# Context's activations and retention's normalised tokens at byte 192 of a 256-byte line

## The chip, the cores and the metric

One core of a Trainium2 chip runs the whole program. The metric is the device time of one execution in microseconds (us); the time before is the median of three runs. The profile is of one further execution of the same program.

## What is computed

Two layers of a diffusion backbone over 512 latent tokens with 256 context tokens, width 1024, all in float32. Layer 0 is windowed attention, layer 1 a bidirectional retention; behind each mixer stands a SwiGLU feed-forward of inner width 2816. Context runs through layer 0 and its feed-forward, and in layer 1 only feeds retention's keys and values.

```python
def swiglu(h, w_in, w_out):
    gate, up = jnp.split(h @ w_in, 2, axis=-1)
    return (jax.nn.silu(gate) * up) @ w_out

...
x = x + mx[5] * swiglu(modulate(rms_norm(x, norm2_g[i]), mx[3], mx[4]), ffn_w_in[i], ffn_w_out[i])
if need_ctx_out:
    y_ctx = y_ctx + mc[2] * out_c
    y_ctx = y_ctx + mc[5] * swiglu(modulate(rms_norm(y_ctx, norm2_g[i]), mc[3], mc[4]),
                                   ffn_w_in[i], ffn_w_out[i])
...
q_x, k_x, v_x, g_x = jnp.split(h_x @ w_qkvg, [qk, 2 * qk, 2 * qk + RET_VWIDTH], axis=-1)
k_c, v_c = jnp.split(h_c @ w_qkvg[:, qk:2 * qk + RET_VWIDTH], [qk], axis=-1)
```

## The kernel before

Every dense product is made from three matmuls (`mm3`, L144): each float32 operand is split into a rounded high part and the remainder, and TensorE adds high x high, low x high and high x low. Numbers on both sides are of the type float32r. So 128 x 128 weights are loaded into the array (an LDWEIGHTS, "PEld" in the profile) for each matmul, and a stream of 128, 256, 384 or 512 columns passes through. Splitting costs a cast on ScalarE and a subtraction on VectorE.

**The first feed-forward** (L970 to L1316). Its 22 inner tiles of 128 features go through in groups of 2, 4, 4, 4, 4, 4. The 768 tokens (512 latent, then 256 context, `WIDE`) are computed in two halves of 384 (`THIRDS`). From the third tile on `seven` (L1129) makes gate and up projection with seven products of 384 columns (L994) on sums of tokens and weights instead of eight. `finish_half` (L1079) multiplies gate and up, writes the rounded half into an `act` tile (ScalarE, L1082) and the remainder behind it (VectorE, L1083). An `act` tile has 2 x 768 columns: high parts of latent and context, then low parts of latent and context. Context's high part stands at column 512 and its low part at column 1280, which are both multiples of 256 bytes.

`output` (L1214) applies the output weights of a finished group while the next group is being made: for each of eight output tiles first the latent tokens (512 columns into the bank pair `pj`, 3 matmuls a tile of the group), then the context tokens (256 columns into `Z`); `out_products` (L1206) takes the high and low parts by the offset `WIDE`. `last_output` (L1227) does the last group in three passes of 256 columns: first latent half, context, second latent half, with the squares for the next norm on ScalarE and, for context, their sums on GpSimd (L211).

**Retention** (L1324 on). Latent tokens are normalised and split into `h_first` and `h_rest` (tiles `aq`, L1334 and L1335) and their sums into `h_sum` (tiles `sA`, L1332); context into tiles `hc` (`context_norm`, L1400, by `norm_mod`, L246). For each of four heads `product_q` (L1408, its matmul L1415) makes queries and keys: the tokens are streamed, 256 columns at a time, over loaded weights. `product_v` (L1419, its matmul L1428) makes values and gates: the tokens are the loaded operand, 128 columns at a time, and 512 columns of weights are streamed. In a head the order on TensorE is: products of `aq` and `hc` by key weights (96 matmuls of L1415), of `sA` (96), of `aq` (24), then the value and gate products of L1428 with `aq`, `hc` and `sA`, in between the scores.

**Where a tile stands.** A pool hands out a partition's bytes in the order of first use. `off_grid(pool, 48)` (L226) takes 48 columns of float32, 192 bytes, so that the tiles after it start 192 bytes past a multiple of 256; `off_grid(pool, 16)` brings it back to the grid with 64 bytes more. Before the change this is done for attention's context tokens (L447), for `h_sum` (L1331) and for the second feed-forward's tokens `hx` (L1783), but not for the first feed-forward's `act`, nor for retention's `aq` and `hc`; these start at byte 0.

Each engine works through its own queue in order. `after(a, b)` (L91) places `a` behind `b` on an engine without a semaphore; `rounded[0]` (L1161) keeps the rounding of a tile's second half behind the next tile's first copy.

Of the kernel before, what the change touches and what calls it, by code (L numbers as in the profile page):

```python
# [9 lines left out]
F32R = mybir.dt.float32r  # L10
# [6 lines left out]
KT = D // P  # L17
SX = 512
SC = 256
# [30 lines left out]
def dit_kernel(ctx, tc, xT, cT, crow, small, consts, masks, tabs0, tabs1, jtab, adaQ, adaN, adaT, wst, out):  # L50
    nc = tc.nc
    mult, add, sub = ALU.mult, ALU.add, ALU.subtract
# [9 lines left out]
    def T(pool, cols, tag, bufs, dt=F32):  # L62
        return pool.tile([P, cols], dt, tag=tag, bufs=bufs, name=tag)

    def pj(n=512):
# [11 lines left out]
    acol = {(l, s, w): cp.tile([P, 8], F32, name=f"acol{l}{s}{w}")  # L77
            for l, s, w in ((0, 0, 0), (0, 1, 0), (0, 0, 1), (0, 1, 1), (1, 0, 0), (1, 1, 0), (1, 0, 1))}
# [12 lines left out]
    def after(ins, others):  # L91
        for o in others:
            tc.add_manual_dep(ins.ins, o.ins.name, order, reason="table set turn")
# [50 lines left out]
    def mm3(o, w, x, first, last, behind=()):  # L144

        whi, wlo = w
        xhi, xlo = x
        after(nc.tensor.matmul(o, whi, xhi, start=first, stop=False), behind)  # L148
        nc.tensor.matmul(o, wlo, xhi, start=False, stop=False)  # L149
        return nc.tensor.matmul(o, whi, xlo, start=False, stop=last)  # L150
# [70 lines left out]
    hpool = [None]  # L221
# [4 lines left out]
    def off_grid(pool, cols):  # L226

        nc.gpsimd.memset(T(pool, cols, "off%d" % cols, 1), 0.0)

    def h_tiles(s):  # L230
        hi = t_h(s)
        if s == 0:
            return hi, t_h(s)
        return hi[:, 0:SC], hi[:, SC:2 * SC]

    def modulate(l, s, which, k, res, h, c=slice(None), t=None, behind=()):
        y = ssq[s][:, c]
        if t is None:
            t = t_hn(y.shape[1])
        after(nc.vector.scalar_tensor_tensor(t, res[k][:, c], acol[l, s, which][:, k:k + 1], y, mult, mult), behind)  # L240
        hi, lo = h[0][:, c], h[1][:, c]
        b = mods[l, s][:, 3 * which, k:k + 1]
        nc.scalar.activation(hi, t, AF.Identity, bias=b)
        return nc.vector.scalar_tensor_tensor(lo, t, b, hi, add, sub)

    def norm_mod(l, s, which, res):  # L246
        h = []
        for k in range(KT):
            h.append(h_tiles(s))
            last = modulate(l, s, which, k, res, h[k])  # L250
        return h, last

    def gated_add(s, l, part, d, o, res):
        return nc.vector.scalar_tensor_tensor(res[d], o, mods[l, s][:, part, d:d + 1], res[d], mult, add)  # L254
# [120 lines left out]
    h, raw = [[], []], []  # L375
# [558 lines left out]
    for g in range(NKV - 1):  # L934
        a, b = make_q(2 * g + 2, behind=() if g else parted), make_q(2 * g + 3)
# [35 lines left out]
    PLAIN, ADA_FROM = 2, 4  # L971
    WIDE = SX + SC
    THIRDS = (slice(0, 384), slice(384, WIDE))
    E = ExitStack()
    ep = E.enter_context(tc.tile_pool(name="ep", bufs=1, reuse_waits="tile"))
    wo_p = A.enter_context(tc.tile_pool(name="wo", bufs=1, reuse_waits="tile"))
# [36 lines left out]
    quarter = lambda: T(hq, 768, "aq", 20, F32R)  # L1013
    parts = lambda t: (t[:, 0:384], t[:, 384:768])
    bank = lambda n: T(psF, 512, n, 2)[:, 0:384]
    fp32 = [T(ep, 2 * WIDE, "act", 5) for _ in range(4)]
    tm = [fp32[k % 4][:, k // 4 * WIDE:(k // 4 + 1) * WIDE] for k in range(KT)]
    A = {(k, 0): parts(T(ep, 768, "aq", 8, F32R)) for k in range(KT)}
    A.update({(k, 1): parts(quarter()) for k in range(KT)})
# [27 lines left out]
    def token_sums():  # L1047

        h1, h2 = THIRDS
        for k in range(4):  # L1050
            t1, t2 = tm[k], tm[k + 4]
            b1, b2 = (mods[0, 0][:, 3, i:i + 1] for i in (k, k + 4))
            stt = nc.vector.scalar_tensor_tensor
            nc.vector.tensor_tensor(t2[:, h2], t1[:, h2], t2[:, h2], op=add)
            stt(t1[:, h2], t1[:, h1], b1, t1[:, h2], add, sub)
            stt(t1[:, h1], t2[:, h2], b1, t1[:, h1], sub, sub)
            stt(park[:, k * 384:(k + 1) * 384], t2[:, h1], b2, t1[:, h1], add, sub)
            for n, t in ((1, t2[:, h2]), (3, t1[:, h2]), (2, t1[:, h1])):
                hi, lo = S[n, k] = parts(quarter())
                ins = nc.scalar.copy(hi, t)  # L1060
                if n == 3:
                    thirds.append(ins)
                nc.vector.tensor_tensor(lo, t, hi, op=sub)  # L1063
# [10 lines left out]
               **{n: (lambda k, n=n: S[n, k]) for n in (1, 2, 3, 4)}}  # L1074

    def new_act():
        return T(ep, 2 * WIDE, "act", 5, F32R)

    def finish_half(a, i, t, up):  # L1079
        nc.vector.tensor_tensor(t, t, up, op=mult)  # L1080
        c = THIRDS[i]
        rounded[0] = nc.scalar.copy(a[:, c], t)  # L1082
        return nc.vector.tensor_tensor(a[:, c.start + WIDE:c.stop + WIDE], t, a[:, c], op=sub)  # L1083

    def project_half(w, i, tag):
        o = bank(tag)
# [37 lines left out]
        if q and f >= ADA_FROM:  # L1124
            ada_tile(*q.pop(0), cr, [behind], fp)

    last_product, copies, rounded, copied_up = [None], [], [None], []

    def seven(middle=None):  # L1129
        g, u = raw_turn(), raw_turn()  # L1130
        l_, r_ = slice(0, 512), slice(512, 1024)
        b11 = w_parts(fp, 1)
        after(nc.scalar.copy(b11[0], g), copied_up if f == PLAIN + 1 else [])
        nc.vector.tensor_tensor(b11[1], g, b11[0], op=sub)
        t1 = T(fp, 512, "bhi", 1, F32R), T(fp, 512, "blo", 1, F32R)
        nc.vector.tensor_tensor(g[:, l_], u[:, l_], g[:, l_], op=sub)
        split(g[:, l_], *t1)
        nc.vector.tensor_tensor(g[:, l_], u[:, r_], g[:, l_], op=sub)
        nc.vector.tensor_tensor(g[:, r_], g[:, r_], g[:, l_], op=sub)
        b24 = w_parts(fp, 1)  # L1140
        high = nc.scalar.copy(b24[0], g)
        half = nc.vector.tensor_tensor(b24[1], g, b24[0], op=sub)
        lows = []
        if middle:
            for ins in thirds:
                after(ins, [high])
            lows = middle()
        nc.vector.tensor_tensor(u[:, l_], u[:, r_], u[:, l_], op=sub)
        b3 = w_parts(fp, 1)
        third = nc.scalar.copy(b3[0], u)  # L1150
        third_low = nc.vector.tensor_tensor(b3[1], u, b3[0], op=sub)
        for ins in lows:
            after(ins, [third_low])
        if cr:
            ada_next(half)
        X, Y, Z = bank("X"), bank("Y"), bank("Z")
        c11, c12, c22, c21 = t_hn(384), t_hn(384), t_sq(384), t_sq(384)
        a = new_act()
        product(Y, operand["11"], b11, 0, True)
        ins = [nc.scalar.copy(c11, Y)]  # L1160
        after(rounded[0], ins)  # L1161
        after(third, ins)
        product(X, operand["12"], b11, 512, True)
        nc.vector.tensor_tensor(c11, c11, X, op=add)
        silu(c11, c11)
        product(Y, operand[2], b24, 0, False)
        copies[:] = [nc.scalar.copy(c12, Y)]
        product(Z, operand[1], t1, 0, True)
        copies.append(nc.scalar.copy(c21, Z))
        product(Y, operand[3], b3, 0, False)  # L1170
        copied_up[:] = [nc.scalar.copy(c22, Y)]
        nc.vector.tensor_tensor(c22, c22, c21, op=add)
        product(Z, operand[4], b3, 512, False)
        nc.vector.tensor_tensor(c12, c12, Z, op=add)
        finish_half(a, 0, c12, c11)
        last_product[0] = product(Y, operand["22"], b24, 512, False)
        silu(c21, Y)
        return a, finish_half(a, 1, c22, c21)
# [27 lines left out]
    def out_products(o, wd, c0, acts, c, step, behind=(), ks=None):  # L1206
        gsz = len(acts)
        for k in ks or range(gsz):
            a, b = divmod(c0 + k * step, 512)
            ws = [x[a][:, b:b + P] if isinstance(x, list) else x[:, c0 + k * step:c0 + k * step + P] for x in wd]  # L1210
            mm3(o, ws, (acts[k][:, c], acts[k][:, c.start + WIDE:c.stop + WIDE]), k == 0, k == gsz - 1,
                () if k else behind)

    def output(acts):  # L1214
# [72 lines left out]
    for gsz in FFN_GROUPS:  # L1287
        acts = []
        for i in range(gsz):
# [4 lines left out]
            else:  # L1294
                a, end = seven(last_sum if f == PLAIN else None)
# [33 lines left out]
    qp = R.enter_context(tc.tile_pool(name="qp", bufs=1, reuse_waits="tile"))  # L1329
    W4 = lambda n: T(psR, 512, n, 2)  # L1330
    off_grid(hS, 48)  # L1331
    h_sum = [(T(hS, 512, "sA", 16, F32R), T(hS, 512, "sA", 16, F32R)) for _ in range(KT)]  # L1332
    off_grid(hS, 16)
    h_first = [T(hpool[0], 512, "aq", 12, F32R) for _ in range(4)]  # L1334
    h_rest = [(T(hpool[0], 512, "aq", 12, F32R), T(hpool[0], 512, "aq", 12, F32R)) for _ in range(4)]  # L1335
    chunk_base = wpos[0]

    def chunk(i, own=False):
# [11 lines left out]
    last_split, hm = [None], []  # L1350
# [47 lines left out]
    h_ctx = []  # L1398

    def context_norm():  # L1400
        h, last = norm_mod(1, 1, 0, cres)
        h_ctx.extend(h)
        return last

    def context_half(i):
# [88 lines left out]
    normed = context_norm()  # L1494
    b11, Yv, vt, ins = values_first(b11)
    rms(0, HALVES[1], bank=pj, behind=[ins])
    for hd in range(RH):
# [18 lines left out]
        k11, k21 = split_chunk(chunk(bq)), split_chunk(chunk(bq + 1))  # L1516
        if hd == 0:
            latent_norm(range(KT), 1)
            sums = token_sums(hm, 0, T(qp, 64, "sh2", 1), h_sum, [normed])
            pieces = []  # L1520
            dx, dcx = strips(0, [sums], pieces)
        cos1, sin1 = rope_tables()
# [26 lines left out]
        else:  # L1549
            k22 = T(qw, 1024, "wx", 4)  # L1550
            ins = nc.vector.tensor_tensor(k22, q22, k11, op=sub)
# [530 lines left out]
```

## Time and profile before

| what | value |
|---|---|
| median of three runs | 1715.1 us (1715.02 to 1717.71) |
| profiled execution, its own time | 1716.71 us |
| its span in the trace | 1714.9 us |
| TensorE busy | 1697.8 us, 99% of the span, 11094 matmuls |
| weight loads | 1530.9 us, 89% |
| VectorE, ScalarE, GpSimd busy | 1338.1, 840.1, 124.2 us |
| granted TensorE clock over the span | 1.0 |
| moved by DMA | 205.67 MB, 120 GB/s |

Two views matter. The groups by shape give a line of the kernel, the engine, the operation, output<-inputs (for a matmul the streamed operand first, the loaded one second), the shape, the count, and after the bar the busy time in us and the mean duration in ns, then the idle time of the engine just before. A matmul's duration holds the time to drain, which overlaps the next one. The timeline gives start (us), duration (us), engine, line, operation; the time from one start to the next is what a matmul takes from its engine.

### The profile page before, as it was taken

The page shows a single profiled execution, that of the slowest core. Times are in us where ns is not written, and L with a number is a line of the kernel's source. Part 1 is how long each engine was busy: PE and PEld are TensorE (multiplying, and loading weights), DVE is VectorE, ACT ScalarE, POOL GpSimd, SP SyncE. Part 2 cuts the span into 40 slices and gives each one's busy share as a digit, 9 for nine tenths or more (in the row PEclk, how much of TensorE's full clock was granted, in tenths as well). Part 3 has the DMA queues.
Part 4 walks back from the last instruction along what each step waited for, and adds up shares of the span by engine and source line. Part 5 has one row for each costly group of instructions (what it writes and reads, how often), then busy time and mean ns, then how long its engine had stood idle before and what let it go on. Part 6 is the DMA issues. An engine that isn't in the chain of part 4 may idle for free.

```text
span 1714.9 us, 28202 instructions
## 1 busy us (share of the span) xinstructions
PE 1697.8 (99%) x11094; PEld 1530.9 (89%) x11094; DVE 1338.1 (78%) x2425; ACT 840.1 (49%) x1509; POOL 124.2 (7%) x268
## 2 busy tenths in 40 slices
PE   8999999999999999999999999999999999999999
PEld 5888878899999999999998898898898999999997
DVE  6798797488778787878799858758768998878774
ACT  5677786264524243343565624525434655445442
POOL 0033443000000000000000000000000100000000
PEclk9999999999999999999999999999999999999999
DMA  9510015233334434343433534433433333233322
GB/s 363 232 38 26 14 40 183 74 124 111 99 127 144 135 112 159 114 144 112 147 101 125 196 98 129 162 105 125 160 99 110 99 99 123 76 122 105 105 75 86
DMA packets 61908, 205.67 MB, mean 120 GB/s; under 512 B 6864, under 2 KB 7760, under 8 KB 61648
## 3 DMA queue, kind: packets, MB, share of 16 engines
q1 hardware_dynamic: 54864, 178.71, 31.2%
q0 software_dynamic: 6912, 25.17, 4.7%
q8 instruction: 87, 1.43, 0.3%
q14 instruction: 45, 0.37, 0.1%
HBM read 201.75 MB, written 2.10 MB: 119 GB/s over the span
## 4 chain that ended last, share of the span: by engine, by line
PE 85%; DVE 8%; DMA 4%; ACT 1%; issue 1%; POOL 0%; SPq 0%; DVEq 0%; ACTq 0%; POOLq 0%
PE Y L994 15%; PE Z L994 8%; PE Z L1428 7%; PE pj L148 7%; PE pj L150 7%; PE pj L149 7%; PE X L994 4%; PE Y L1415 3%; PE pO L809 2%; PE pT L784 2%; PE S L764 2%; PE pj L1428 2%; PE X L1415 2%; DMA adan<-in_adaQ_dram 1%; PE Z L150 1%; PE Z L149 1%
## 5 line engine op out<-in xcount | busy, mean ns | idle before, releaser
L994 PE MATMUL Y<-aq,whi 128*128 128x384 f32 x640 | 173.3, 335 | 0.0
L254 DVE SCALAR_TENSOR_TENSOR res<-pj,mod,res 128x512 f32<-128x512 f32 (+1 forms) x102 | 74.4, 731 | 57.2 <-PE pj L150 56.7
L994 PEld LDWEIGHTS Y<-aq,whi 128*128 128x128 f32 x640 | 116.5, 188 | 0.7 <-DVE aq L1063 0.3
L140 ACT CAST whi<-wraw 128x1024 fp32r<-128x1024 f32 x75 | 78.4, 1050 | 68.8 <-PE Z L150 27.5
L141 DVE TENSOR_TENSOR wlo<-wraw,whi 128x1024 fp32r<-128x1024 f32 x75 | 91.5, 1224 | 20.7 <-ACT whi L140 20.0
L994 PE MATMUL Y<-aq,wlo 128*128 128x384 f32 x320 | 106.9, 334 | 0.0
L274 DVE CUSTOM_DVE_ANT_0 y<-adaw,crow,small_sb 128x1024 bf16<-128x1024 f32 x64 | 81.9, 1280 | 17.5 <-DMA adaw<-in_adaT_dram 17.5
L1345 ACT CAST whi<-wraw 128x1024 fp32r<-128x1024 f32 x55 | 57.5, 1050 | 68.5 <-PE Y L150 52.5
L1428 PE MATMUL Z<-whi,sA 128*128 128x512 f32 x256 | 80.7, 391 | 0.0
L1346 DVE TENSOR_TENSOR wlo<-wraw,whi 128x1024 fp32r<-128x1024 f32 x55 | 66.9, 1224 | 15.8 <-ACT whi L1345 15.7
L101 ACT ACTIVATE pr<-pr,stat,qs 128x513 f32<-128x513 f32 (+2 forms) x96 | 74.1, 776 | 10.0 <-DVE stat L771 7.2
L778 POOL TENSOR_SCALAR pr<-pr,stat 128x512 f32<-128x512 f32 (+2 forms) x96 | 67.3, 707 | 72.0 <-DVE stat L777 51.5
L148 PE MATMUL pj<-ax,whi 128*128 128x512 f32 x176 | 68.8, 391 | 0.9 <-DVE res L254 0.6
L150 PE MATMUL pj<-ax,whi 128*128 128x512 f32 x176 | 68.6, 390 | 0.0
L149 PE MATMUL pj<-ax,wlo 128*128 128x512 f32 x176 | 68.5, 389 | 0.0
L271 POOL DMA_DIRECT2D adaw<-in_adaT_dram x48 | 25.6, 533 | 510.1 <-DVE mod L274 411.1
L148 PE MATMUL pj<-act,whi 128*128 128x512 f32 (+1 forms) x156 | 60.2, 386 | 0.3 <-DVE res L254 0.3
L994 PEld LDWEIGHTS Y<-aq,wlo 128*128 128x128 f32 x320 | 60.1, 188 | 0.0
L149 PE MATMUL pj<-act,wlo 128*128 128x512 f32 (+1 forms) x156 | 59.9, 384 | 0.0
L994 PE MATMUL Y<-sA,whi 128*128 128x256 f32 x304 | 59.9, 281 | 0.0
L150 PE MATMUL pj<-act,whi 128*128 128x512 f32 (+1 forms) x156 | 59.5, 381 | 0.0
L765 DVE CUSTOM_DVE_ANT_0 pr<-S,mask,qs 128x256 f32<-128x256 f32 (+1 forms) x96 | 52.9, 565 | 7.8 <-PE S L764 5.9
(626 smaller groups left out, 5573.5 us busy)
## 6 DMA issues: line engine op xcount, KB each, us to landing
wraw<-in_wst_dram SPq DMA_DIRECT2D x231, 512.0 KB, 3.6
adaw<-in_adaT_dram POOLq DMA_DIRECT2D x48, 512.0 KB, 3.9
wx<-in_wst_dram SPq DMA_DIRECT2D x28, 512.0 KB, 4.4
adan<-in_adaQ_dram SPq DMA_DIRECT2D x16, 512.0 KB, 6.6
adan<-in_adaN_dram SPq DMA_DIRECT2D x16, 512.0 KB, 8.7
res<-in_xT_dram SPq DMA_DIRECT2D x16, 256.0 KB, 5.1
q<-in_adaN_dram SPq DMA_DIRECT2D x16, 256.0 KB, 4.0
aq<-in_adaN_dram SPq DMA_DIRECT2D x12, 256.0 KB, 5.5
```

The costliest lines, as they stand in the source:

```text
L101: ins = nc.scalar.activation(*args, **kw)
L140: after(nc.scalar.copy(hi, raw), behind)
L141: after(nc.vector.tensor_tensor(lo, raw, hi, op=sub), low)
L148: after(nc.tensor.matmul(o, whi, xhi, start=first, stop=False), behind)
L149: nc.tensor.matmul(o, wlo, xhi, start=False, stop=False)
L150: return nc.tensor.matmul(o, whi, xlo, start=False, stop=last)
L254: return nc.vector.scalar_tensor_tensor(res[d], o, mods[l, s][:, part, d:d + 1], res[d], mult, add)
L274: tiled.append(nc.vector.tensor_tensor_reduce(junk, w, cr[:, s * 1024:(s + 1) * 1024], 1.0, sm_t[:, C_ADAB + l * 48 + j:C_ADAB + l * 48 + ...
L778: nc.gpsimd.tensor_scalar(pt[:, :n], pt[:, :n], st[:, 6 + e:7 + e], 1.0, op0=mult, op1=mult)
L994: ins = nc.tensor.matmul(o, p, r, start=first and k + i == 0, stop=k == 3 and i == 2, skip_group_check=not first)
L1415: ins = nc.tensor.matmul(o[:, e * SC:(e + 1) * SC], p[:, ws], r, start=first and k + e + i == 0, stop=k == 3 and i == 2, skip_group_check= ...
L1428: ins = nc.tensor.matmul(o, p, r, start=first and k + i == 0, stop=k == 3 and i == 2, skip_group_check=not first)
```

## The change

`act` tiles become 1600 columns (`ACT`, 25 x 256 bytes) and hold latent high, latent low, 48 columns of nothing, context high, context low, 16 columns of nothing; context so starts at byte 192 (column 1072). `act_parts` gives high and low parts. The second half of the tokens holds 128 latent and 256 context columns, whose places are no longer next to each other, so `finish_half` rounds and subtracts it in two pieces; `rounded` is now a list. `fp32`, the first four of these tiles, is used earlier for the unsplit tokens and only grows.

In retention `off_grid(hpool[0], 48)` stands ahead of `h_first`, and context's tiles (`hc_room`) are taken right behind `h_rest`; `norm_mod` falls away, its loop is in `context_norm`. The 64-column tile `sh2` falls away, and `token_sums` uses `acol[0, 0, 0]`, which layer 0 is done with.

In the built program TensorE's queue is the same matmul by matmul. The operands that move from byte 0 to byte 192 are: streamed, 528 matmuls of `act` with 256 columns and 480 of L1415 (288 with `aq`, 192 with `hc`); loaded, 480 of L1428 (288 with `aq`, 192 with `hc`). No other matmul operand changes its byte within 256. On VectorE and ScalarE 22 instructions more stand in the first feed-forward, one for each tile; on GpSimd there are two memsets more.

```diff
-    def norm_mod(l, s, which, res):
-        h = []
-        for k in range(KT):
-            h.append(h_tiles(s))
-            last = modulate(l, s, which, k, res, h[k])
-        return h, last
...
+    CTX = 2 * SX + 48
+    ACT = CTX + 2 * SC + 16
...
-    fp32 = [T(ep, 2 * WIDE, "act", 5) for _ in range(4)]
+    fp32 = [T(ep, ACT, "act", 5) for _ in range(4)]
...
     def new_act():
-        return T(ep, 2 * WIDE, "act", 5, F32R)
+        return T(ep, ACT, "act", 5, F32R)
+
+    def act_parts(a, c):
+
+        if c.start < SX:
+            return a[:, c], a[:, c.start + SX:c.stop + SX]
+        return a[:, CTX:CTX + SC], a[:, CTX + SC:CTX + 2 * SC]
 
     def finish_half(a, i, t, up):
         nc.vector.tensor_tensor(t, t, up, op=mult)
-        c = THIRDS[i]
-        rounded[0] = nc.scalar.copy(a[:, c], t)
-        return nc.vector.tensor_tensor(a[:, c.start + WIDE:c.stop + WIDE], t, a[:, c], op=sub)
+        cs = (THIRDS[0],) if i == 0 else (slice(384, SX), slice(SX, WIDE))
+        pieces = [(t[:, c.start - 384 * i:c.stop - 384 * i], *act_parts(a, c)) for c in cs]
+        rounded[:] = [nc.scalar.copy(hi, src) for src, hi, _ in pieces]
+        for src, hi, lo in pieces:
+            ins = nc.vector.tensor_tensor(lo, src, hi, op=sub)
+        return ins
...
-        after(rounded[0], ins)
+        for r in rounded:
+            after(r, ins)
...
-            mm3(o, ws, (acts[k][:, c], acts[k][:, c.start + WIDE:c.stop + WIDE]), k == 0, k == gsz - 1,
+            mm3(o, ws, act_parts(acts[k], c), k == 0, k == gsz - 1,
                 () if k else behind)
...
     off_grid(hS, 16)
+    off_grid(hpool[0], 48)
     h_first = [T(hpool[0], 512, "aq", 12, F32R) for _ in range(4)]
     h_rest = [(T(hpool[0], 512, "aq", 12, F32R), T(hpool[0], 512, "aq", 12, F32R)) for _ in range(4)]
+    hc_room = [T(hpool[0], 512, "hc", 8, F32R) for _ in range(KT)]
+    off_grid(hpool[0], 16)
...
     def context_norm():
-        h, last = norm_mod(1, 1, 0, cres)
-        h_ctx.extend(h)
+        for k, t in enumerate(hc_room):
+            h_ctx.append((t[:, 0:SC], t[:, SC:2 * SC]))
+            last = modulate(1, 1, 0, k, cres, h_ctx[k])
         return last
...
-            sums = token_sums(hm, 0, T(qp, 64, "sh2", 1), h_sum, [normed])
+            sums = token_sums(hm, 0, acol[0, 0, 0], h_sum, [normed])
```

On ScalarE this is the place where the first `seven` begins, behind the two plain tiles: `hn` and `sq` hold the activations, `act` the tile, `wraw` and `whi` weights before and after rounding. Before:

```order
349 L165 CAST aq<-crow 128x384 x3
350 L1160 COPY hn<-Y 128x384
351 L1082 CAST act<-hn 128x384
352 L1150 CAST whi<-wraw 128x1024
353 L165 CAST aq<-crow 128x384
354 L140 CAST whi<-wraw 128x1024
355 L1167 COPY hn<-Y 128x384
```

And now:

```order
350 L165 CAST aq<-crow 128x384 x3
351 L1164 COPY hn<-Y 128x384
352 L1084 CAST act<-hn 128x128
353 L1084 CAST act<-hn 128x256
354 L165 CAST aq<-crow 128x384
355 L1154 CAST whi<-wraw 128x1024
356 L140 CAST whi<-wraw 128x1024
357 L1172 COPY hn<-Y 128x384
```

The cast of a second half is two, and here one cast of a token sum comes ahead of the weights' cast (L1150, now L1154); in the later `seven` the rows keep their order, with two casts for one.

GpSimd at the end of the first feed-forward and in `last_output`; `adaw` are the weights of the second layer's modulation, `y` the sum of squares of context, `off` the columns of `off_grid`. Before:

```order
92 L271 DMA adaw<-in_adaT_dram 128x1024 x48
93 L211 TENSOR_TENSOR y_9307<-y_9307,sq 128x256 x7
94 L228 MEMSET off_9600 128x48
95 L228 MEMSET off_9618 128x16
96 L211 TENSOR_TENSOR y_13934<-y_13934,sq 128x256 x3
```

And now:

```order
92 L264 DMA adaw<-in_adaT_dram 128x1024 x48
93 L228 MEMSET off_9664 128x48
94 L228 MEMSET off_9686 128x16
95 L211 TENSOR_TENSOR y_9351<-y_9351,sq 128x256 x7
96 L228 MEMSET off_9644 128x48
97 L228 MEMSET off_9662 128x16
```

The two new memsets come ahead of the seven additions of context's squares.

More of the change, by code (lines that the diff above doesn't have):

```diff
@@ L1125, in ada_next @@
             ada_tile(*q.pop(0), cr, [behind], fp)
-    last_product, copies, rounded, copied_up = [None], [], [None], []
+    last_product, copies, rounded, copied_up = [None], [], [], []
     def seven(middle=None):
```

## The prediction

> **What bounds the kernel now.** I read the page first: busy shares, the granted clock, the chain.
>
> ```profile
> span 1714.9 us, 28202 instructions
> PE 1697.8 (99%) x11094; PEld 1530.9 (89%) x11094; DVE 1338.1 (78%) x2425; ACT 840.1 (49%) x1509; POOL 124.2 (7%) x268
> PEclk9999999999999999999999999999999999999999
> PE 85%; DVE 8%; DMA 4%; ACT 1%; issue 1%; POOL 0%; SPq 0%; DVEq 0%; ACTq 0%; POOLq 0%
> ```
>
> TensorE is busy for 99% of the span and holds 85% of the chain that ended last, at an unthrottled clock. The change removes no matmul, so it can only alter how long each one takes, or make TensorE wait. The next view is therefore TensorE's groups by shape, for products that stream 256 columns (the operand named first streams, the second is loaded as weights).
>
> ```profile
> L994 PE MATMUL Y<-sA,whi 128*128 128x256 f32 x304 | 59.9, 281 | 0.0
> L1415 PE MATMUL Y<-sA,whi 128*128 128x256 f32 x256 | 44.3, 276 | 0.0
> L150 PE MATMUL Z<-act,whi 128*128 128x256 f32 x156 | 44.1, 283 | 0.0
> L1415 PE MATMUL Y<-aq,whi 128*128 128x256 f32 x128 | 24.3, 283 | 0.1
> ...
> L1415 PE MATMUL X<-hc,whi 128*128 128x256 f32 x128 | 23.7, 283 | 0.0
> ```
>
> Same shape, same weights, three durations. `act`, `aq` and `hc` start at byte 0 of a 256-byte line here and take 283 ns; `sA` starts at byte 192 (L1331) and takes 276 or 281. So the byte does matter, but byte 192 has two paces. These durations hold a tail that overlaps the next matmul; what counts is from start to start, in the timeline. First, `output` of the first feed-forward: 12 context matmuls, 12 latent ones of 512 columns, the next context run.
>
> ```profile
> 487.53 0.28 PE L148 MATMUL Z<-act,whi 128*128 128x256 f32 x1
> ...
> 488.97 0.40 PE L148 MATMUL pj<-act,whi 128*128 128x512 f32 x1
> ...
> 490.13 0.39 PE L150 MATMUL pj<-act,whi 128*128 128x512 f32 x1
> 490.35 0.39 PE L148 MATMUL pj<-act,whi 128*128 128x512 f32 x1
> ...
> 491.71 0.28 PE L148 MATMUL Z<-act,whi 128*128 128x256 f32 x1
> ```
>
> Context at byte 0: 1.44 us for 12, **120 ns** each. The last six latent ones take 1.36 us, 226.7 ns each, but the first six 1.38 (488.97 to 490.35): a run at byte 0 leaves its successor some 0.02 us of delay. One round is 4.18 us.
>
> Next, a run at byte 192 that follows settled 512-column matmuls (second feed-forward, L994), at its head and at its tail 336 matmuls later:
>
> ```profile
> 1475.01 0.28 PE L994 MATMUL Y<-hx,whi 128*128 128x256 f32 x1
> ...
> 1476.42 0.28 PE L994 MATMUL Z<-sA,whi 128*128 128x256 f32 x1
> ...
> 1514.59 0.39 PE L148 MATMUL pj<-ax,whi 128*128 128x512 f32 x1
> 1514.81 0.39 PE L149 MATMUL pj<-ax,wlo 128*128 128x512 f32 x1
> 1515.04 0.39 PE L150 MATMUL pj<-ax,whi 128*128 128x512 f32 x1
> ```
>
> Twelve take 1.41 us, **117.5 ns** each, from the first one on; over the whole run 39.58 us for 336, 117.8; and the 512s behind it start at their settled 226 ns. I call this the wide pace. The third place is retention, head 1, where a run at byte 0 (`aq`, `hc`: 96) passes into byte 192 (`sA`: 96) and back (`aq`: 24):
>
> ```profile
> 1008.30 0.39 PE L150 MATMUL Y<-qk,whi 128*128 128x512 f32 x1
> 1008.53 0.28 PE L1415 MATMUL Y<-aq,whi 128*128 128x256 f32 x1
> ...
> 1020.04 0.29 PE L1415 MATMUL Y<-sA,whi 128*128 128x256 f32 x1
> ...
> 1030.94 0.28 PE L1415 MATMUL Y<-aq,whi 128*128 128x256 f32 x1
> ...
> 1033.80 0.40 PE L1428 MATMUL X<-whi,aq 128*128 128x512 f32 x1
> ```
>
> 96 in 11.51 us (119.9 ns), then 96 in 10.90 (**113.5**, the close pace), then 24 in 2.86. So the close pace is seen where a byte-192 run follows a byte-0 run of 256 columns; after settled 512s the wide pace is seen, and it stays. That difference decides what the change is worth. Last, byte 192 on the other operand: product_v (L1428) streams 512 columns of weights and loads the tokens; first `hc` at byte 0, then `sA` at byte 192.
>
> ```profile
> 1039.27 0.39 PE L1428 MATMUL pj<-whi,hc 128*128 128x512 f32 x1
> ...
> 1044.70 0.39 PE L1428 MATMUL Z<-whi,sA 128*128 128x512 f32 x1
> ...
> 1085.69 0.39 PE L1428 MATMUL Z<-whi,sA 128*128 128x512 f32 x1
> ...
> 1096.68 0.39 PE L1428 MATMUL Z<-whi,aq 128*128 128x512 f32 x1
> ```
>
> 24 in 5.43 us (226.3 ns) against 48 in 10.99 (229.0). As the loaded operand, byte 192 is dearer by 2.3 ns than the settled 226.7.
>
> **The change part by part.** Minus is faster.
>
> Context's part in `output`: 432 matmuls, each run behind settled 512s, so the wide pace. A round becomes 12 x 0.1175 + 12 x 0.2267 = 4.13 us against 4.18: -0.05, for 32 rounds -1.6; the 8 rounds of the two-tile group (6 + 6) give 6 x 0.0025 + 0.02 each, -0.3. Not every run is followed by 512s (each group's last by 384s), so I take **-1.8**. At the close pace it would be about -2.9; where no pace changes, 0.
>
> Context's part in `last_output`: 96 matmuls at 120 ns, of which some follow a byte-0 run of 256 (113.5) and some a rest: between -0.2 and -0.6, **-0.4**.
>
> Retention's streamed tokens: per head `aq` and `hc` come to byte 192 and so all 216 matmuls of the stretch above stand there. It begins behind settled 512s (the L150 row at 1008.30), so the whole of it should run wide, the 96 `sA` too, which lose their close pace: 216 x 0.1176 = 25.40 us against the 25.27 of the rows (1008.53 to 1033.80). +0.13 a head, **+0.5** for four. At the close pace it is 24.52, -0.75 a head, -3.0. That is the largest open term.
>
> Retention's loaded tokens: 480 matmuls of L1428 (288 `aq`, 192 `hc`) go to byte 192: 480 x 2.3 ns = +1.1; four runs lose the 0.02 us left by the byte-0 run ahead: **+1.0**. From below 0, were the 2.3 ns due to `sA`'s place and not its byte; by the two counts above (229.0 - 226.3) +1.3.
>
> The split round-off: the second half of each `seven` now has two casts on ScalarE and two subtractions on VectorE.
>
> ```profile
> L1082 ACT CAST act<-sq 128x384 fp32r<-128x384 f32 x22 | 11.4, 516 | 0.0
> L1042 ACT ACTIVATE act<-act,mod 128x256 f32<-128x256 f32 x8 | 3.6, 501 | 0.0
> L1042 ACT ACTIVATE act<-act,mod 128x128 f32<-128x128 f32 x8 | 2.8, 390 | 0.0
> ```
>
> By the nearest rows 0.50 + 0.39 - 0.52, at most +0.37 us on ScalarE for each of 22 tiles, and something like it on VectorE. Who waits for it is seen in one `seven`, engine by engine:
>
> ```profile
> 550.00 0.52 ACT L1082 CAST act<-sq 128x384 fp32r<-128x384 f32 x1
> 550.42 1.05 ACT L1150 CAST whi<-wraw 128x1024 fp32r<-128x1024 f32 x1
> ...
> 552.24 1.22 DVE L1151 TENSOR_TENSOR wlo<-wraw,whi 128x1024 fp32r<-128x1024 f32 x1
> ...
> 555.92 0.48 ACT L1169 COPY sq<-Z 128x384 f32<-128x384 f32 x1 [1.18 <-PE Z L994]
> ```
>
> Queued behind the cast on ScalarE is L1150 (b3's high part), then L1151 on VectorE (its low part, done at 553.46). b3 is used first by the product after the one that L1169 copies out, at 555.9: 2.4 us of cover. So 0; without the cover 20 x 0.37 = +7.4. The tiles themselves are read by `output` a tile later.
>
> The two added memsets stand on GpSimd ahead of the context's squares in `last_output`.
>
> ```profile
> 852.81 0.73 POOL L211 TENSOR_TENSOR y<-y,sq 128x256 f32<-128x256 f32 x1 [17.85 <-ACT sq L210]
> ```
>
> They wait for the last product's readers of the room; GpSimd idles 17.85 us there: 0. `sh2` in another tile, and context_norm's room taken earlier: 0, the same instructions.
>
> Sum: -1.8 - 0.4 + 0.5 + 1.0 = **-0.7 us**. The profiled execution took 1716.7 (1.8 around its span) and would take 1716.0; the median of the runs shown, 1715.1, becomes **1714.4**.
>
> A rule speaks against any effect at all: the Trainium skill, "TensorE: Matmul & The Clock Gate", section "Step-by-step: what each phase is for", gives TensorE two independent read ports into SBUF, one for the streamed operand and one for the weights; by it no byte would slow the other and the sum would be 0. The trace does not agree: 119.9 and 113.5 ns in one stretch of L1415.
>
> **The rivals.**
>
> *Close pace in retention.* If the 216-run settles at 113.5 instead of 117.6: -1.8 - 0.4 - 3.0 + 1.0 = -4.2, 1710.9; with `output` close as well -2.9 - 0.6 - 3.0 + 1.0 = -5.5, 1709.6. For: L1415's `sA` runs so now, in just this code. Against: the L994 run, which enters from 512s as this one will, keeps wide for 336 matmuls. 0.22.
>
> *Close pace in `output` alone:* -2.9 - 0.6 + 0.5 + 1.0 = -2.0, 1713.1. 0.08.
>
> *No effect of the byte,* each pace belonging to its code: 1715.1. Two paces inside L1415 speak against it. 0.05.
>
> *Slower: the split delays the weights.* Each `seven` of the first feed-forward, ScalarE at L1150: if the cover were smaller than the added 0.37 us, TensorE would wait up to that in 20 of them: -0.7 + 7.4 = +6.7, 1721.8; it decides only once b3's low part ends after 555.9, 2.4 us later than now. 0.07, with 0.03 for a dearer loaded operand (another 7 ns each, +3.4).
>
> **How the numbers follow.** My forecast, wide pace throughout, has 0.55. About 0.2% (3.4 us) can be told from no change by a measurement of this kernel. Faster by more is the close pace in retention, 0.22; slower by more 0.10; the rest, 0.55 + 0.08 + 0.05, is 0.68. The range goes down past 1710.9 to 1710.5 and up to 1717.5, the forecast with the loaded operand and `last_output` at their dear ends and the spread of the runs shown (to 1717.7); it leaves out both paces close, and the delayed weights.
>
> **What would show it.** Right: in `output` the context group's duration falls from 283 to about 281 and a round to 4.13 us; in head 1 the first L1415 to the first L1428 takes about 25.4 us with `sA` at 281, not 276; L1428 with `hc` takes 229 ns a matmul. Wrong: `aq` and `hc` at 276; L1428 at 226.7; any idle time of TensorE on `act`, L1150 or L1151's successors in the first feed-forward.

## The result and the profile after

The changed kernel is slower: 1719.49 us in the median of 18 runs (1717.99 to 1721.02) against 1715.84 for the kernel before, in 18 runs (1714.68 to 1719.07). The ratio is 1.0020, its 95% interval 1.0013 to 1.0026, so the loss is 2.2 to 4.5 us. The forecast was 1714.4, with a range from 1710.5 to 1717.5.

First the page of the changed kernel: its span, the busy times, and the shares of the chain that ended last.

```profile
span 1716.2 us, 28245 instructions
PE 1699.7 (99%) x11094; PEld 1531.2 (89%) x11094; DVE 1341.2 (78%) x2447; ACT 841.8 (49%) x1531; POOL 125.0 (7%) x270
PE 89%; DVE 7%; ACT 2%; DMA 1%; issue 1%; POOL 0%; SPq 0%; ACTq 0%; DVEq 0%; POOLq 0%
```

Nothing stands out here. TensorE has the same 11094 matmuls and the same 99%. The spans differ by only 1.3 us, in the main because the one profiled execution of before lost 1.0 to 1.5 us in its first 60 us which neither the changed kernel's trace nor any of the eight experiments' traces shows; that difference is not the change's. So the traces were laid side by side matmul by matmul (TensorE's queue is the same in both), and the time from one start to the next was compared place by place.

**Where the prediction looked.** The timeline of the changed kernel at the round of `output` that the prediction showed (487.53 us of before stands at 484.82 here), and one row of the groups by shape:

```profile
484.82 0.28 PE L148 MATMUL Z<-act,whi 128*128 128x256 f32 x1
...
486.23 0.39 PE L148 MATMUL pj<-act,whi 128*128 128x512 f32 x1
...
487.59 0.39 PE L148 MATMUL pj<-act,whi 128*128 128x512 f32 x1
...
488.95 0.28 PE L148 MATMUL Z<-act,whi 128*128 128x256 f32 x1
```

```profile
L150 PE MATMUL Z<-act,whi 128*128 128x256 f32 x156 | 43.8, 281 | 0.0
```

Twelve context matmuls take 1.41 us (117.5 ns each, 120 before), the six 512s behind them 1.36 (1.38 before), the round 4.13 (4.18). Head 1 of retention, first its streamed tokens (L1424 is the former L1415), then the loaded ones (L1437, the former L1428):

```profile
1004.44 0.28 PE L1424 MATMUL Y<-aq,whi 128*128 128x256 f32 x1
...
1015.74 0.28 PE L1424 MATMUL Y<-sA,whi 128*128 128x256 f32 x1
...
1027.05 0.28 PE L1424 MATMUL Y<-aq,whi 128*128 128x256 f32 x1
...
1029.88 0.40 PE L1437 MATMUL X<-whi,aq 128*128 128x512 f32 x1
...
1035.39 0.39 PE L1437 MATMUL pj<-whi,hc 128*128 128x512 f32 x1
...
1040.88 0.39 PE L1437 MATMUL Z<-whi,sA 128*128 128x512 f32 x1
```

96 matmuls in 11.30 us, 96 in 11.31, 24 in 2.83: 25.44 us in all (25.27 before, 25.40 forecast), all at the wide pace, `sA` too. `hc` as the loaded operand: 24 in 5.49 us, 228.8 ns each (226.3 before). All this is as forecast.

**Where it did not look.** Between the end of retention and the second feed-forward's first output product. The timeline, TensorE's row that ends retention (it streams `qk`) and the first row that streams `ax`; of before, then of the changed kernel:

```profile
1367.42 0.28 PE L150 MATMUL Y<-qk,whi 128*128 128x256 f32 x1
1367.54 0.29 PE L148 MATMUL X<-hx,wx 128*128 128x256 f32 x1
...
1401.53 0.39 PE L148 MATMUL pj<-ax,whi 128*128 128x512 f32 x1
```

```profile
1364.37 0.28 PE L150 MATMUL Y<-qk,whi 128*128 128x256 f32 x1
1365.29 0.38 PE L148 MATMUL X<-hx,wx 128*128 128x256 f32 x1 [0.64 <-ACT hx L243]
...
1402.71 0.39 PE L148 MATMUL pj<-ax,whi 128*128 128x512 f32 x1
```

The same matmuls take 34.11 us before and 38.34 now: **+4.23 us**, where the change touches no operand. I call this span the passage. Two rows of the timeline say who was late: VectorE's first write of `hm` (the second feed-forward's normalised tokens, ahead of their splitting into `hx`), and ScalarE's first `hx` behind it.

```profile
1364.21 0.88 DVE L240 SCALAR_TENSOR_TENSOR hm<-res,acol,y 128x256 f32<-128x256 f32 x2 [4.58 <-PE Y L149]
1364.73 0.91 ACT L243 ACTIVATE hx<-hm,mod 128x256 fp32r<-128x256 f32 x2 [4.45 <-DVE hm L240]
```

In before the same VectorE row has no bracket, so no wait:

```profile
1362.60 0.97 DVE L240 SCALAR_TENSOR_TENSOR hm<-res,acol,y 128x256 f32<-128x256 f32 x2
```

In before VectorE writes `hm` 4.8 us ahead of TensorE's last `qk` product (1362.60 and 1367.42), in after 0.16 us ahead of it (1364.21 and 1364.37). In after it waits 4.58 us for a product that makes nothing it reads. `Y` is only the name of the tile that the product writes; what VectorE waits for is that the product has *read* `qk`, because `hm` now lies in `qk`'s bytes. The places in the two built programs (bytes of a partition):

| tile | before | after |
|---|---|---|
| `aq` | 171776 to 196352 | 171712 to 196288 |
| `qk` (retention's output operand at its end) | 196352 to 212736 | **212736 to 229120** |
| `hc` (no longer read by then) | 212736 to 229120 | 196288 to 212672 |
| `hm`, in the pool opened next | **212736 to 229120** | **212736 to 229120** |

A pool hands out bytes by first use. Before, `hc`'s first use is in `context_norm`, behind `qk`'s; the change takes `hc_room` right behind `h_rest`, ahead of `qk`. So `hc` and `qk` change places, and `hm`, which lay over dead `hc`, lies over live `qk`.

What that costs TensorE is poorly seen in busy time. Engine by engine, two stretches of 9 us, first in before, then in after. Behind the stretch and its length stand the busy time in us and, in brackets, the number of instructions of PE, PEld, VectorE, ScalarE and GpSimd; the last three numbers are the granted clock, the share of DMA and its GB/s.

```profile
1358.00:1367.00 9.00, 9.00 (x76) 8.95 (x75) 6.96 (x19) 5.18 (x13) 3.56 (x8) 1.00 0.55 180
1367.00:1376.00 9.00, 8.93 (x74) 8.55 (x74) 9.00 (x19) 5.88 (x12) 2.27 (x3) 1.00 0.21 64
```

```profile
1358.00:1367.00 9.00, 8.33 (x65) 7.73 (x64) 3.93 (x11) 2.51 (x7) 2.46 (x7) 1.00 0.32 117
1367.00:1376.00 9.00, 7.81 (x50) 6.27 (x49) 9.00 (x18) 7.04 (x14) 2.99 (x4) 1.00 0.09 26
```

PE's busy time falls by only 1.8 us (17.93 to 16.14), but its matmuls fall from 150 to 115: 35 fewer, at 0.12 us each 4.2 us. A matmul that is held up is shown longer (0.38 us at 1365.29, 0.28 where it runs freely), and the page calls that busy.

By place, after minus before: first feed-forward -2.3 us, of which 0.7 are two stalls at 413 and 416 us (of the three experiments that leave `act` alone two lack most of them and one, e7_hc_swapped, has them in full, so they come and go without the change), so -1.6; `last_output` -0.35; from there to the end of retention +1.3; the passage +4.2. Together +3.6, as the medians have it (+3.65). Not counted are the first 60 us and the stretch from there to 405 us, which is 0.4 us shorter in after; no matmul operand that the change moves is read there, and the experiments' traces lie between -0.4 and +0.5 us of before in it.

### The profile page after: what moved, and what is told of

The parts are those of the page before. It is cut to its first block, busy times and chain, and to the rows that moved or that the text cites. A ratio compares the mean times of both kernels' runs of the same rounds, so it can differ in the third digit from the quotient of the medians.

```text
span 1716.2 us, 28245 instructions
## 1 busy us (share of the span) xinstructions
PE 1699.7 (99%) x11094; PEld 1531.2 (89%) x11094; DVE 1341.2 (78%) x2447; ACT 841.8 (49%) x1531; POOL 125.0 (7%) x270
## 3 DMA queue, kind: packets, MB, share of 16 engines
q8 instruction: 87, 1.43, 0.3%
## 4 chain that ended last, share of the span: by engine, by line
PE 89%; DVE 7%; ACT 2%; DMA 1%; issue 1%; POOL 0%; SPq 0%; ACTq 0%; DVEq 0%; POOLq 0%
PE Y L989 15%; PE Z L989 8%; PE Z L1437 7%; PE pj L148 7%; PE pj L150 7%; PE pj L149 7%; PE X L989 4%; PE Y L1424 3%; PE S L757 2%; PE pO L802 2%; PE pT L777 2%; PE pj L1437 2%; PE X L1424 1%; PE Z L148 1%; PE Z L149 1%; PE Z L150 1%
## 5 line engine op out<-in xcount | busy, mean ns | idle before, releaser
L1437 PE MATMUL Z<-whi,sA 128*128 128x512 f32 x256 | 80.7, 392 | 0.0
```

Of the source, the lines that this page charges most:

```text
L1437: ins = nc.tensor.matmul(o, p, r, start=first and k + i == 0, stop=k == 3 and i == 2, skip_group_check=not first)
```

## The experiments

The room theory: the whole loss is `hm`'s (or `hx`'s) wait for products that read `qk`; the moved operands do what the prediction said, about -0.6 in all. The byte theory, the rival: the new places of the operands cost the time, by a price that was not foreseen, and the wait only shows it. All times are against the kernel before, run beside them.

| kernel | median, us | before | ratio (95%) | passage, us |
|---|---|---|---|---|
| changed kernel | 1719.49 | 1715.84 | 1.0020 (1.0013 to 1.0026) | 38.34 |
| e1_room_back | 1719.30 | 1716.36 | 1.0019 (1.0010 to 1.0028) | 37.36 |
| e2_room_only | 1720.07 | 1716.36 | 1.0026 (1.0016 to 1.0036) | 39.18 |
| e3_act_only | 1715.33 | 1716.36 | 0.9992 (0.9983 to 1.0001) | 34.22 |
| e4_hc_only | 1718.88 | 1716.36 | 1.0014 (1.0006 to 1.0023) | 37.40 |
| e6_pools_swapped | 1716.11 | 1716.45 | 0.9998 (0.9989 to 1.0007) | 34.27 |
| e7_hc_swapped | 1715.33 | 1716.45 | 0.9995 (0.9986 to 1.0004) | 34.87 |
| e8_act_hc_swapped | 1713.74 | 1716.45 | 0.9986 (0.9977 to 0.9995) | 34.30 |
| e9_act_128 | 1717.18 | 1716.45 | 1.0005 (0.9996 to 1.0014) | 35.05 |

Before's passage is 34.11. Without any wait on `qk` it varies by up to 0.9 us (e9_act_128, e7_hc_swapped); that spread I did not follow up, and it is small beside the 3.3 to 5.1 of the kernels that wait.

**The room alone, on the kernel before (e2_room_only).**

```diff
+    hc_room = [T(hpool[0], 512, "hc", 8, F32R) for _ in range(KT)]
...
-        h, last = norm_mod(1, 1, 0, cres)
-        h_ctx.extend(h)
+        for k, t in enumerate(hc_room):
+            h_ctx.append((t[:, 0:SC], t[:, SC:2 * SC]))
+            last = modulate(1, 1, 0, k, cres, h_ctx[k])
```

> The kernel before with one thing done: hc's room is taken ahead of qk's, so that hm lies over qk. No operand of a matmul changes its byte within its 256. The room theory: hm's first write waits about 4.6 us for the products that read qk, TensorE has its idle time at hx behind it, and the kernel is about 4.2 us slower than before (1719 to 1720 where before is 1715 to 1716). The byte theory: within 0.5 us of before.

Measured: 1.0026, 2.7 to 6.2 us slower, and the passage 5.07 us longer. VectorE's row in its timeline:

```profile
1364.90 0.88 DVE L240 SCALAR_TENSOR_TENSOR hm<-res,acol,y 128x256 f32<-128x256 f32 x2 [4.58 <-PE Y L149]
```

The same 4.58 us as in the changed kernel, with not one operand at another byte of its line. The order of two rooms is enough to make the loss.

**The changed kernel with the rooms in their old order (e1_room_back).**

```diff
-    off_grid(hS, 16)
-    off_grid(hpool[0], 48)
...
-    hc_room = [T(hpool[0], 512, "hc", 8, F32R) for _ in range(KT)]
     off_grid(hpool[0], 16)
+    qk_room = [T(hpool[0], 512, "qk", 8, F32) for _ in range(KT)]
+    off_grid(hpool[0], 48)
+    hc_room = [T(hpool[0], 512, "hc", 8, F32R) for _ in range(KT)]
+    nc.gpsimd.memset(T(hpool[0], 16, "offb", 1), 0.0)
...
-                hm.append(t_qk(F32))
+                hm.append(qk_room[k])
```

> The changed kernel with the retention pool laid out in the old order again (aq, qk, hc), so that the second feed-forward's hm lies over hc, which is dead by then, and no longer over qk. Every operand that the change moved to byte 192 stays there. The room theory (the change lost its time where hm's first write waits for the last products that read qk, and only there): that write has no wait on TensorE, the 4.23 us between 1367 and 1400 us of before's time are gone, and the kernel stands 0.5 to 1.5 us below before, by the terms that the two traces give elsewhere (first feed-forward -2.3 with two stalls, last_output -0.35, retention +1.3). The byte theory (the new places of the operands cost the time, and the wait at hm only shows it): the kernel stays 3 us above before, since every operand stands where the change put it.

Measured: 1.0019, as slow as the changed kernel. By the number the byte theory was right and mine had fallen. The timeline says otherwise: `hm` has no wait, and the next instruction but one has it.

```profile
1360.02 0.97 DVE L240 SCALAR_TENSOR_TENSOR hm<-res,acol,y 128x256 f32<-128x256 f32 x2
1360.91 0.70 DVE L1376 TENSOR_TENSOR sh<-mod 128x4 f32<-128x4 f32 x1
1364.76 0.48 DVE L244 SCALAR_TENSOR_TENSOR hx<-hm,mod,hx 128x256 fp32r<-128x256 f32 x1 [3.14 <-PE Y L149]
```

The two pads around `hc` add 256 bytes to a pool whose top is fixed, so `qk` had slid down to 196096, and the tiles `hx` end at 196288: the last of them lay in the first `qk`. The experiment had moved the collision, not taken it away, and so its time decides nothing between the two theories.

**`hc` alone at byte 192 (e4_hc_only).** It holds the same error as the one above.

```diff
+    qk_room = [T(hpool[0], 512, "qk", 8, F32) for _ in range(KT)]
+    off_grid(hpool[0], 48)
+    hc_room = [T(hpool[0], 512, "hc", 8, F32R) for _ in range(KT)]
+    off_grid(hpool[0], 16)
...
-                hm.append(t_qk(F32))
+                hm.append(qk_room[k])
...
```

> The kernel before with the context's normalised tokens hc alone at byte 192; the latent tokens aq stay at byte 0 and the rooms in their old order. Rule of neighbours (a run of 256-column matmuls at byte 192 takes 113.5 ns each where the run ahead of it is one at byte 0, and 117.8 where it isn't): hc's streamed runs, which follow aq's at byte 0, take 113.5 ns in place of 120.0, the loaded ones 2.3 ns more each; about 0.8 us below before. Rule of the place alone (117 ns at byte 192 whatever stands ahead): streamed runs at 117, and within 0.5 us of before.

Measured: 1.0014, a loss where both rules of the pace had a gain or nothing. Its waits from 1340 to 1400 us (engine, line waited for, us in total, times, longest):

```profile
DVE hx L244 <- PE Y L149: 3.7, 1, 3.7
```

`qk` lies at 196096 here too, and the passage takes 37.40 us. Outside it the pace is as the rule of neighbours has it (below, where it is measured cleanly).

**The changed kernel with the next two pools in the other order (e6_pools_swapped).** Nothing in the retention pool is altered. The pool of the second feed-forward's weights is opened ahead of that of `hm`, so that the weights lie over `qk` (as before the change) and `hm` over dead `hc`.

```diff
-        hM, hW, hX = (ctx.enter_context(tc.tile_pool(name=n, bufs=1, reuse_waits="tile", side="right"))
-                      for n in ("hM", "hW", "hX"))
+        hW, hM, hX = (ctx.enter_context(tc.tile_pool(name=n, bufs=1, reuse_waits="tile", side="right"))
+                      for n in ("hW", "hM", "hX"))
```

> The changed kernel, with every operand and the whole retention pool where the change put it, and one thing changed: of the second feed-forward's pools, the one of weights is opened ahead of the one of hm, so that the weights lie over qk (as they do in the kernel before) and hm over hc, which is dead. In the run with the old order of rooms, qk had slid 256 bytes down into the place of the last hx, and the same wait stood there (3.1 us); here nothing of qk lies under hm or hx. The room theory: no wait on the retention output's products at hm or hx, the stretch from 1367 to 1400 us as long as before's 32.64 within 0.3, and the whole 0.5 to 1.5 us below before. The byte theory: 2 to 3 us above before as in the two kernels with the same bytes.

Measured: 0.9998 (-1.9 to +1.2 us), by the median 0.3 us below before where 0.5 to 1.5 were expected; its interval doesn't meet the changed kernel's (1.0013 and up). VectorE and TensorE in its timeline:

```profile
1360.19 0.97 DVE L240 SCALAR_TENSOR_TENSOR hm<-res,acol,y 128x256 f32<-128x256 f32 x2
...
1361.71 0.47 DVE L244 SCALAR_TENSOR_TENSOR hx<-hm,mod,hx 128x256 fp32r<-128x256 f32 x1
...
1365.02 0.28 PE L150 MATMUL Y<-qk,whi 128*128 128x256 f32 x1
1365.14 0.29 PE L148 MATMUL X<-hx,wx 128*128 128x256 f32 x1
...
1399.29 0.39 PE L148 MATMUL pj<-ax,whi 128*128 128x512 f32 x1
```

No wait, the passage 34.27 us. All operands stand where the change put them, and the loss is gone: the byte theory falls. Together with the room alone, which makes the loss without a moved operand, the cause is shown from both sides.

**The activations alone (e3_act_only).** The kernel before with the change's `CTX`, `ACT`, `act_parts` and `finish_half`, nothing of retention.

```diff
+    CTX = 2 * SX + 48
+    ACT = CTX + 2 * SC + 16
...
-            mm3(o, ws, (acts[k][:, c], acts[k][:, c.start + WIDE:c.stop + WIDE]), k == 0, k == gsz - 1,
+            mm3(o, ws, act_parts(acts[k], c), k == 0, k == gsz - 1,
```

> The kernel before with the first feed-forward's half of the change alone: the context's part of each activation at byte 192, latent first. Nothing of retention is changed. By the two traces: the context matmuls of the output products run at 117.8 ns in place of 119.3, the first 36 of last_output's at 113.9; 1.6 us less, or 2.3 with the two stalls at 413 and 416 us that only before's trace has, and 0.35 in last_output: 2.0 to 2.7 us below before, no wait at hm. The prediction as it stands on record has -2.2 for these two terms. Rival: half of the gain is a run's chance in where stalls fall, and it is 0 to 1 us below before.

Measured: 0.9992 (-2.9 to +0.2), 1.4 us in the ratio, less than the 2.0 to 2.7 expected. From 405 to 837 us of before its trace is 2.0 us shorter, of which 0.5 are the two stalls at 413 and 416 us, shorter here than in before: 1.5 for the change. In `last_output` a gain of 0.36 was eaten by two held matmuls (0.37). The direction is as forecast; the interval alone doesn't exclude zero.

**`hc` alone, without the collision (e7_hc_swapped).** `hc` stands between `aq` and `qk`, and the two pools are swapped as above.

```diff
+    off_grid(hpool[0], 48)
+    hc_room = [T(hpool[0], 512, "hc", 8, F32R) for _ in range(KT)]
+    off_grid(hpool[0], 16)
...
-        h, last = norm_mod(1, 1, 0, cres)
-        h_ctx.extend(h)
+        for k, t in enumerate(hc_room):
...
-                      for n in ("hM", "hW", "hX"))
+                      for n in ("hW", "hM", "hX"))
```

> The kernel before with the context's normalised tokens hc alone at byte 192, and hm kept off qk by the same swap of the two pools (the first run with hc alone at byte 192 had qk slide into the place of hx, and a wait of 3.7 us there, which hid its own term). hc's streamed runs 113.7 ns in place of 120.0 (192 of them: -1.2 us), the loaded ones 229.0 in place of 226.9 (+0.4): 0.8 us below before, no wait at hm or hx. The byte theory: 2 us above before, as measured with hc there.

Measured: 0.9995 (-2.4 to +0.7), no wait on `qk`. Head 1 in its timeline, the first rows of each run (`aq` at byte 0, `hc` and `sA` at 192, `aq` at 0):

```profile
1006.72 0.28 PE L1419 MATMUL Y<-aq,whi 128*128 128x256 f32 x1
...
1012.48 0.29 PE L1419 MATMUL X<-hc,whi 128*128 128x256 f32 x1
...
1017.93 0.28 PE L1419 MATMUL Y<-sA,whi 128*128 128x256 f32 x1
...
1028.82 0.28 PE L1419 MATMUL Y<-aq,whi 128*128 128x256 f32 x1
...
1031.68 0.40 PE L1432 MATMUL X<-whi,aq 128*128 128x512 f32 x1
```

48 in 5.76 us (120.0 ns), 48 in 5.45 (113.5), 96 in 10.89 (113.4), 24 in 2.86: 24.96 us against 25.27 before and 25.44 in the changed kernel. `hc` behind a run at byte 0 takes the close pace, and keeps it for `sA`. The whole by its rows: 192 x -6.3 ns = -1.2, and 192 x 2.1 = +0.4.

**Both (e8_act_hc_swapped).**

```diff
+    CTX = 2 * SX + 48
+    ACT = CTX + 2 * SC + 16
...
+    off_grid(hpool[0], 48)
+    hc_room = [T(hpool[0], 512, "hc", 8, F32R) for _ in range(KT)]
+    off_grid(hpool[0], 16)
...
-                      for n in ("hM", "hW", "hX"))
+                      for n in ("hW", "hM", "hX"))
```

> The version that the runs so far point to: the activations' context at byte 192 (measured alone: 1.0 us below before in the median, 2.2 by its stretches) and hc at byte 192 behind aq at byte 0 (0.8 by its rows), hm off qk. If the two add up: 1.8 to 3.0 us below before, and below each of them alone. If something else than the room costs time in retention: not under the kernel with the activations alone.

Measured: 0.9986 (0.9977 to 0.9995), 0.9 to 3.9 us faster than before: the two add up, and this version is faster than both kernels, if by little. `aq` stays at byte 0.

**Another byte (e9_act_128).** The activations alone, with context at byte 128.

```diff
-    CTX = 2 * SX + 48
-    ACT = CTX + 2 * SC + 16
+    CTX = 2 * SX + 32
+    ACT = CTX + 2 * SC + 32
```

> The kernel with the activations' change alone, but the context's part at byte 128 in place of 192. If it counts only that the place is not byte 0: the context matmuls of the output products at 117.8 ns and the same 1 to 2 us below before. If it is byte 192 alone that helps: 119.3 ns as before and the time of before within 0.5 us, or, should byte 128 be worse than 0, above 120 ns. No run so far has a streamed operand at byte 128, so neither has the better evidence.

Measured: 1.0005 (-0.7 to +2.4). The round of `output` that stands at 487.53 in before:

```profile
486.54 0.28 PE L148 MATMUL Z<-act,whi 128*128 128x256 f32 x1
...
487.97 0.39 PE L148 MATMUL pj<-act,whi 128*128 128x512 f32 x1
...
489.36 0.39 PE L148 MATMUL pj<-act,whi 128*128 128x512 f32 x1
...
490.74 0.28 PE L148 MATMUL Z<-act,whi 128*128 128x256 f32 x1
```

1.43 us for the twelve (119.2 ns), 1.39 for the six 512s behind them, 4.20 for the round: no better than byte 0 (4.18), where byte 192 has 4.13. Being off byte 0 is not what helps; of the three bytes tried, 192 alone does.

## Why the prediction was wrong

**The step that failed** is the sentence "`sh2` in another tile, and context_norm's room taken earlier: 0, the same instructions." The instructions are the same, but a room taken earlier is another place, and a place decides whom the next pool's first writer waits for. The step looked at what the moved line does and not at what comes to lie where, three stages later. It could have been seen ahead of any run, in the places of the tiles in the built program. Where it put 0 the runs show +4.2 us in the changed kernel, from VectorE's wait of 4.58 us at `hm`, and that alone turns -0.6 into +3.6. The signs that the prediction listed for being right in `output` and in head 1 all came: none of them looked behind retention. None of the rivals held this mechanism: the slower ones spoke of delayed weights in the first feed-forward and of a dearer loaded operand.

**Context in `output`**, forecast -1.8: -1.6, at the wide pace throughout, a round 4.13 us as worked out. **`last_output`**, forecast -0.4: -0.35. The first 36 matmuls take 113.9 ns, the 60 behind the norm's small products 118.

**Retention's streamed tokens**, forecast +0.5 for four heads: +0.17 in each of heads 1 to 3, where the forecast had 0.13. Head 0 was wrong: its `aq` and `hc` run at the close pace. Timeline of the changed kernel:

```profile
890.21 0.39 PE L1437 MATMUL pj<-whi,hc 128*128 128x512 f32 x1
890.44 0.28 PE L1424 MATMUL Y<-aq,whi 128*128 128x256 f32 x1
...
901.34 0.28 PE L1424 MATMUL Y<-sA,whi 128*128 128x256 f32 x1
```

96 in 10.90 us, 113.5 ns, 0.6 us less than before's. Waits for split weights among the `sA` products behind them (one matmul is 0.75 us from start to start) took it back: from the first `aq` product to the last run of `aq` it is 23.00 us against 22.90. The price was near for three heads; the fourth came out even by chance: e1_room_back and e6_pools_swapped, with the same bytes, need 25.34 and 25.33 us for the 216 matmuls of head 0, where the changed kernel needs 25.86 and before 25.87.

**Retention's loaded tokens**, forecast +1.0: matmul against matmul, `aq` 227.6 to 229.4 ns and `hc` 226.9 to 229.0, together +0.9.

**The split round-off**, forecast 0 behind 2.4 us of cover: from 405 to 837 us no place is slower, and what waited for the casts in the changed kernel is VectorE alone, 21 times for 16.7 us in all (27 times for 22.0 us before), as it must wait to subtract:

```profile
who waited for it (us, times):
  DVE act L1086: 16.7, 21
```

**The two memsets**, forecast 0: `last_output` is faster, and no engine waits for them there.

So the terms for the operands summed to -0.7 and came to -0.6; the kernel with the pools swapped is 0.3 us faster in the median (0.6 lies well inside its interval). The rivals by the close pace had 0.30 between them and fell, but for head 0. The prediction also weighed a rule of the Trainium skill ("TensorE: Matmul & The Clock Gate", section "Step-by-step: what each phase is for": two independent read ports) and drew from it that no byte would matter. That conclusion is not borne out: with context at byte 0, 128 and 192, a round of `output` takes 4.18, 4.20 and 4.13 us. It also went further than the section, which says that the two ports do not slow each other and nothing of where in a line an operand starts; no run here tests the ports themselves.

## What to carry to other kernels

In a pool that gives out bytes by first use, taking a room earlier is a move of memory: before it is priced at nothing, write down which live tile each first write of the next pool falls on, and whose reads it must wait for. A wait on a product whose result the waiter never reads is the mark of that. And an experiment that shifts tiles must be looked at in the same table, or it moves the collision and seems to refute the right cause.

## What the runs showed of the hardware

The pace of a run of 256-column matmuls at byte 192 depends on what it enters from, and it lasts. It is 113.5 ns behind a run at byte 0, and also (head 0 of the changed kernel) behind 512-column products whose *loaded* operand stands at byte 192; it is 117.8 behind 512-column products with both operands at byte 0, for 216 matmuls without a break. A wait can reset it, to either. Behind the waits among the `sA` products of head 0 the rest of the run takes 117.8 ns in the changed kernel and 113.5 in e6_pools_swapped; and in the latter a hold of 0.06 us ahead of them had turned the close pace into 118. What in the chip keeps the two paces apart, and what decides which of them a wait leaves, no run here shows.

Context at byte 128 is no better than at byte 0 in `output` (119.6 ns against 119.3 over the 430 matmuls that were compared), byte 192 is (117.8). Byte 64 was not tried.
